# Plain k-tiles between the pair operations of a group, and a fifth pair of buffers for split weights

## The chip, the cores and the metric

The kernel runs on one core of a Trainium2 chip. The metric is the device time of one execution in microseconds (us); it took 2559.11 us in the median of three runs (2558.76 to 2559.23). TensorE (PE) multiplies matrices, VectorE (DVE) and ScalarE (ACT) work elementwise, GpSimd (POOL) does little here, and SyncE (SP) issues the loads of the weights. Each engine executes its own instructions in the order in which they stand.

## The reference

Two transformer blocks follow one another on 256 tokens of width 2048, everything in float32. The change touches the output projection and the gated feed-forward network (FFN) of the first block:

```
D_FF = -(-8 * D_MODEL // (3 * 256)) * 256          # 5632
...
        mixed = g_a * (y_a @ w_branch_a[l]) + g_b * (y_b @ w_branch_b[l])
        h = h + mixed @ w_out[l]

        hn = rmsnorm(h, ffn_norm[l])
        h = h + (jax.nn.silu(hn @ w_gate[l]) * (hn @ w_up[l])) @ w_down[l]
    return rmsnorm(h, final_norm)
```

Ahead of it stand the first block's norm, input projection and two attentions; behind it the whole second block, which the change leaves as it is.

## The kernel before

**Products in three passes.** A float32 operand is split into a high half (rounded to the fast float32r type) and a low half (what is left), and a product is taken as high x high + high x low + low x high: three matmuls. For weights, `high` (L449) makes the high half `wh` on ACT, and `low` (L453) the low half `wl` on DVE, each on a tile of 128 x 1024.

**The stream of weights.** `STREAM` lists all weight tiles in the order of use. `fetch` loads a tile into one of six `raw` buffers, in order on SP's queue. `divide` splits the next one; `fill` keeps `look` split tiles ready ahead of the one in use (2 in the output projection, 3 in the FFN), in four pairs of `wh` and `wl` buffers. `low` of a tile is recorded one tile after its `high`.

**A group** (`group_t`, matmuls on L578) makes 1024 output columns for all 256 tokens in four blocks: two halves of the tokens by two halves of the columns, in eight PSUM banks. The stage has 19 groups: two of the output projection (`out`), then in three parts 4, 4 and 3 groups of gate and up (`gu`), each part followed by two groups of `down`. A k-tile is 128 rows of the weights. For four of the k-tiles, taken as two pairs, a group forms the 2 x 2 x 2 block product with seven products instead of eight, in the manner of Strassen and Winograd. These seven operations (`OPS`: B11, B22, t1, t3, t2, B21, t4) have 6 matmuls each; `t1`, `t3`, `t2` and `t4` need a sum of two weight tiles first, which DVE makes in place (L431). The other k-tiles (12 in most groups, 8 in the last two) are plain: 12 matmuls and one split tile each, four products that accumulate into the banks B21, B22, t4 and std.

In the kernel before, a group runs its seven operations first and all plain k-tiles after them. When `t4` is recorded, `early` takes the banks B11, t1, t3 and t2 into sums (L616 on ACT, L617 to L620 on DVE; in `out` and `down` these are added to the residual `h`, L632); after the last plain k-tile `late` adds the other four banks (L1156 in `gu`, L636 in `out` and `down`). Then the roles of the banks are permuted (`map`), so that the next group opens in banks which `early` has freed.

**Tasks.** Small work between groups is held in generators that are resumed every 2400 ns of recorded matmul work: `turned` transposes a group's result four 128 x 128 blocks at a time (L649) into one bank, `self.one`, and hands it to `done`, which evacuates it as split operands (L478, L479, L481, L482). For `gu`, `gated` first multiplies silu(gate) by up (L1128, L1129). A task is brought to its end by `finish`: after the next group in `out` and `gu`, before the last four k-tiles in `down`.

A scheduler then puts the recorded instructions of each engine into their final order, by priority and by when it expects them to be ready.

Of the kernel before, what the change touches and what calls it, by code (L numbers as in the profile page):

```python
# [14 lines left out]
ALU = mybir.AluOpType  # L15
# [15 lines left out]
OUT_PAIRS = ((0, 1), (2, 3))  # L31
GU_PAIRS = ((0, 4), (1, 5))
DOWN_PAIRS = ((0, 1), (2, 3))
# [16 lines left out]
DV_COLS = ((0, 330), (330, 676), (676, 1024))  # L50


def weight_plan():
    plan = []

    def unit(key, *segs):
        plan.append((key, segs))
# [9 lines left out]
    def tgroup(key, w, kts, pairs, col):  # L67


        kts = list(kts)  # L70
        w1, w2 = (w, w) if isinstance(w, str) else w
        c1 = [(col, col + 512)]
        c2 = [(col + 512, col + 1024)] if isinstance(w, str) else c1
        for c in range(0, len(pairs), 2):
# [5 lines left out]
        rest = [k for i, k in enumerate(kts) if not any(i in p for p in pairs)]  # L80
        for i in range(0, len(rest), 2):
            unit(key + ("std", i), *[x for k in rest[i:i + 2] for x in ((w1, [k], c1), (w2, [k], c2))])

    for c in range(8):
        unit(("lat", c), ("w_in", [2 * c, 2 * c + 1], [(3072, 3840)]))
# [25 lines left out]
    for j in range(2, 16):  # L111
        if j < 10:
            h = j - 2
# [27 lines left out]
    for p, (i0, n) in enumerate(PARTS):  # L141
# [7 lines left out]
    return plan  # L149


def _width(ranges):
    return sum((b if a is None else b - a) for a, b in ranges)


PLAN = weight_plan()
# [6 lines left out]
OPS = ("B11", "B22", "t1", "t3", "t2", "B21", "t4")  # L163

ROLES = {"B11": 0, "B22": 1, "t1": 2, "t3": 3, "t2": 4, "B21": 5, "t4": 6, "std": 7}
EARLY, LATE = (0, 2, 3, 4), (1, 5, 6, 7)


def stream():

    out, u = [], 0
    while u < len(PLAN):
        key, n = PLAN[u][0], UNIT_COLS[u]
        if key[0] == "lat":
            u += 1
        elif "pair" in key:
            out += [(op, u, n // 2) for op in OPS]
            u += 2
        else:
            cuts = [n // 2, n] if key[0] in ("va", "dv") else [min(a + 1024, n) for a in range(0, n, 1024)]  # L180
            out += [(u, a, b) for a, b in zip([0] + cuts, cuts)]
            u += 1
    return out


# [66 lines left out]
class Norm:  # L252

    r = B = None
# [14 lines left out]
class Prog:  # L269
# [282 lines left out]
        nc.vector.tensor_tensor(o[:, 1], f, o[:, 0].bitcast(F32), op=ALU.subtract)  # L552
        return o

    def group_t(self, key, xs, cs, pairs, early, late, extra=None):

        nc = self.nc  # L560
        n = len(xs)
        paired = {k for p in pairs for k in p}
        rest = [k for k in range(n) if k not in paired]
        b = {}
        place = lambda r: self.psp.tile([P, 512], F32, tag=f"bank{self.map[ROLES[r]]}", name="q", bufs=1)
        self.one = self.map[7]
        left = dict.fromkeys(OPS, 3 * len(pairs))
        std = (("B21", "B22"), ("t4", "std"))
        left["std"] = 0
        for r in std[0] + std[1]:  # L570
            left[r] += 3 * len(rest)
# [12 lines left out]
        for c in range(0, len(pairs), 2):  # L584
            for op in OPS:
                p, wh, wl = self.take()
                assert p[0] == op and PLAN[p[1]][0] == key + ("pair", c, 0), (key, p)
                self.fill()
                for i, (ka, kb) in enumerate(pairs[c:c + 2]):
                    w = [h[:, 512 * i:512 * i + 512] for h in (wh, wl)]  # L590
                    cmb = lambda m: (cs[c + i][:, 0, m, :], cs[c + i][:, 1, m, :])
                    x = {"B11": lambda: cut(xs[ka], t0), "B21": lambda: cut(xs[kb], t0), "B22": lambda: cmb(2),
                         "t4": lambda: cut(xs[kb], t1), "t1": lambda: cmb(0), "t2": lambda: cmb(1),
                         "t3": lambda: cmb(3)}[op]()
                    product(op, x, w)
        if pairs:
            early(b)
        self.one = self.map[4]
        for i, k in enumerate(rest):
            if extra:  # L600
                extra(k)
            p, wh, wl = self.take()
            assert PLAN[p[0]][0][:len(key)] == key, (key, p)
# [472 lines left out]
    def block1_out(self, mixed, cm):  # L1076

        nc = self.nc
# [16 lines left out]
        task = None  # L1095
        for g in range(2):
            early, late = self.residual(h, g)
            self.group_t(("out", g), mixed, cm, OUT_PAIRS, early, late)
            if task:
                self.finish(task)  # L1100
# [6 lines left out]
            task = self.add(self.turned(src, 8, (lambda g: lambda i, x: done(8 * g + i, x))(g), 3), urgent=True)  # L1107
        m = self.small()
        nc.vector.reduce_sum(m, ss, axis=AX.X)
        nh = Norm()  # L1110
# [3 lines left out]
    def block1_ffn(self, h, hn, cs, nh, th):  # L1114
# [30 lines left out]
        for p, (i0, n) in enumerate(PARTS_T):  # L1145
            acts, ca, task = [], [], th
            for g in range(i0 // 4, (i0 + n) // 4):
                sb_ = []

                def early(b):  # L1150
                    sb_.extend(self.sums(b))

                def late(b):
                    for i, r in enumerate(self.LATE_OF):
                        if sb_:
                            nc.vector.tensor_tensor(sb_[i], b[r], sb_[i], op=ALU.add)  # L1156
                        else:
                            sb_.append(b[r])

                self.group_t(("gu", g), hn, cs, GU_PAIRS, early, late)  # L1160
                self.finish(task)
# [3 lines left out]
            t0, need = task, n - 4  # L1165
            for g in range(2):
                early, late = self.residual(h, g)
                operands = Acts(acts, n)
                self.group_t(("down", p, g), operands, ca, DOWN_PAIRS, early, late,
                             lambda k: k >= need and self.finish(t0))  # L1170
                if last:
                    src = [h[t][:, 1024 * g:1024 * g + 1024] for t in range(2)]

# [373 lines left out]
    def build(self):  # L1547
        nc, tc, t = self.nc, self.tc, self.t
        with ExitStack() as ctx:
# [20 lines left out]
            with ExitStack() as c0:  # L1570
# [94 lines left out]
```

## Time and profile before

| | us |
|---|---|
| median of three runs | 2559.11 |
| the profiled execution | 2559.29 |
| its span | 2557.5 |
| PE busy (matmuls) | 2495.7 (98%) |
| weight loads of PE (PEld) | 2129.2 (83%) |
| DVE busy | 1841.6 (72%) |
| ACT busy | 1366.4 (53%) |
| stage of the groups, first to last matmul | 522.3 to 1361.8 |

A row of the profile names line, engine, operation, output and inputs, shapes and a count; in square brackets stands the idle time of the engine ahead of it and what ended that. Matmuls overlap, so one lasts longer than the interval between two.

### The profile page before, as it was taken

Reading aid. Unit: us, or ns where it says so; the run is one execution under the profiler, and the core shown is the slowest. Engines: PE = TensorE matmul, PEld = TensorE weight load, DVE = VectorE, ACT = ScalarE, POOL = GpSimd, SP = SyncE. Lnnn points to the kernel's source line nnn. Section 1 sums busy time; section 2 is a strip of 40 time slices with the busy share of each in tenths; the row PEclk is TensorE's granted clock in tenths of the full one; section 3 lists DMA queues with packets and bytes.
Section 4 is the critical chain, followed back from the end, with each engine's and each line's share of the span. In section 5 each row is a group of like instructions: output and inputs, shape, how many; then the busy total and the mean of one; then the engine's idle time right before and its main releaser. Section 6 shows DMA issues by size and latency. Waiting matters only on the chain.

```text
span 2557.5 us, 35199 instructions
## 1 busy us (share of the span) xinstructions
PE 2495.7 (98%) x13218; PEld 2129.2 (83%) x13218; DVE 1841.6 (72%) x2617; ACT 1366.4 (53%) x2036; POOL 119.3 (5%) x134
## 2 busy tenths in 40 slices
PE   9999999999999999999998999999999999999997
PEld 8988888877877777787777888888788888888886
DVE  8867766888787877878786578665876566656765
ACT  6555565556554454545456545555655455545553
POOL 3000000000000000000004000002200000000002
PEclk9999999999999999999999999999999999999998
DMA  6644455556555564565644544455455555555552
GB/s 235 202 153 146 165 180 183 189 198 207 172 181 201 169 204 167 184 210 170 205 166 144 197 164 157 146 190 175 148 188 183 190 190 190 184 193 191 186 176 91
DMA packets 131723, 458.46 MB, mean 179 GB/s; under 512 B 14624, under 2 KB 17056, under 8 KB 131296
## 3 DMA queue, kind: packets, MB, share of 16 engines
q1 hardware_dynamic: 130608, 452.78, 52.6%
q10 hardware_dynamic: 944, 3.43, 0.4%
q8 instruction: 103, 1.69, 0.3%
q14 instruction: 68, 0.56, 0.1%
HBM read 454.06 MB, written 2.10 MB: 178 GB/s over the span
## 4 chain that ended last, share of the span: by engine, by line
PE 85%; DVE 10%; issue 2%; ACT 2%; DMA 0%; POOL 0%; POOLq 0%; ACTq 0%; SPq 0%; DVEq 0%
PE acc L494 33%; PE q L578 23%; PE acc L495 17%; DVE wl L453 4%; PE acc L492 2%; PE acc L527 2%; PE acc L526 2%; PE acc L528 1%; DVE raw L431 1%; PE acc L491 1%; ACT wh L449 1%; PE ms L770 1%; DVE ft L1156 1%; DVE hl L482 1%; PE ms L1326 1%
## 5 line engine op out<-in xcount | busy, mean ns | idle before, releaser
L453 DVE TENSOR_TENSOR wl<-raw,wh 128x1024 fp32r<-128x1024 f32 (+4 forms) x939 | 1116.0, 1198 | 536.4 <-ACT wh L449 532.8
L449 ACT ACTIVATE wh<-raw 128x1024 fp32r<-128x1024 f32 (+4 forms) x939 | 961.5, 1032 | 813.2 <-PE acc L494 344.2
L494 PE MATMUL acc<-hl,wh 128*128 128x512 f32 x3746 | 1327.3, 397 | 7.4 <-DVE hl L482 6.5
L495 PE MATMUL acc<-hl,wl 128*128 128x256 f32 x3746 | 1049.0, 281 | 0.7 <-DVE wl L453 0.7
L494 PEld LDWEIGHTS acc<-hl,wh 128*128 128x128 f32 x3746 | 703.5, 188 | 166.9 <-DVE hl L482 6.0
L495 PEld LDWEIGHTS acc<-hl,wl 128*128 128x128 f32 x3746 | 708.2, 189 | 9.2 <-DVE wl L453 2.0
L578 PE MATMUL q<-wh,hl 128*128 128x512 f32 x1988 | 628.4, 392 | 18.5 <-ACT wh L449 17.9
L578 PEld LDWEIGHTS q<-wh,hl 128*128 128x128 f32 x1988 | 372.0, 188 | 107.5 <-ACT wh L449 30.8
L578 PE MATMUL q<-wl,hl 128*128 128x512 f32 x994 | 388.6, 391 | 0.9 <-DVE wl L453 0.8
L578 PEld LDWEIGHTS q<-wl,hl 128*128 128x128 f32 x994 | 186.7, 188 | 41.7 <-DVE wl L453 2.6
L657 ACT ACTIVATE ev<-acc 128x256 f32<-128x256 f32 x288 | 106.3, 384 | 182.6 <-PE acc L492 181.3
L690 POOL TENSOR_TENSOR ssq<-ssq,sq 128x256 f32<-128x256 f32 x77 | 74.9, 982 | 1562.1 <-ACT sq L680 1560.4
L660 DVE TENSOR_TENSOR tmp<-acc,ev 128x256 f32<-128x256 f32 x257 | 101.4, 422 | 60.0 <-ACT ev L657 59.8
L492 PE MATMUL acc<-hl,wh 128*128 128x512 f32 x288 | 108.3, 396 | 0.0
L578 PE MATMUL q<-wh,combo 128*128 128x512 f32 x304 | 100.8, 396 | 4.2 <-ACT wh L449 4.2
L526 PE MATMUL acc<-wh,hl 128*128 128x512 f32 (+4 forms) x264 | 94.0, 356 | 2.8 <-ACT hl L481 2.3
L527 PE MATMUL acc<-wl,hl 128*128 128x512 f32 (+4 forms) x264 | 91.0, 346 | 3.1 <-DVE wl L453 2.4
L431 DVE TENSOR_TENSOR raw<-raw 128x1024 f32<-128x1024 f32 x76 | 92.8, 1221 | 1.3
L528 PE MATMUL acc<-wh,hl 128*128 128x512 f32 (+4 forms) x264 | 89.4, 344 | 0.6 <-DVE hl L482 0.6
L491 PE MATMUL acc<-hl,wl 128*128 128x256 f32 x288 | 82.9, 288 | 0.0
L578 PEld LDWEIGHTS q<-wh,combo 128*128 128x128 f32 x304 | 57.1, 188 | 19.1 <-ACT wh L449 6.6
L578 PE MATMUL q<-wl,combo 128*128 128x512 f32 x152 | 60.7, 399 | 0.2 <-DVE wl L453 0.2
(275 smaller groups left out, 1625.0 us busy)
## 6 DMA issues: line engine op xcount, KB each, us to landing
raw<-in_w_dram SPq DMA_DIRECT2D x801, 512.0 KB, 4.0
raw<-in_w_dram SPq DMA_DIRECT2D x18, 384.0 KB, 3.2
raw<-in_w_dram SPq DMA_DIRECT2D x16, 362.0 KB, 4.2
raw<-in_w_dram SPq DMA_DIRECT2D x16, 346.0 KB, 3.4
raw<-in_w_dram SPq DMA_DIRECT2D x15, 256.0 KB, 3.6
raw<-in_w_dram SPq DMA_DIRECT2D x8, 364.0 KB, 3.8
raw<-in_w_dram SPq DMA_DIRECT2D x8, 348.0 KB, 3.7
x<-in_xT_dram SPq DMA_DIRECT2D x8, 256.0 KB, 5.8
```

What stands on the lines that cost most here:

```text
L431: self.nc.vector.tensor_tensor(raw[:, :n], parts[a][:, :n], parts[b][:, :n], op=ALU.add)
L449: self.nc.scalar.activation(wh[:, :n], raw[:, :n], AF.Copy)
L453: self.nc.vector.tensor_tensor(wl[:, :n], raw[:, :n], wh[:, :n].bitcast(F32), op=ALU.subtract)
L491: nc.tensor.matmul(acc[:, S:], wl, x[:, 0, :], start=False, stop=False)
L492: nc.tensor.matmul(acc, wh, x, start=False, stop=True)
L494: nc.tensor.matmul(acc, wh, x, start=first, stop=False)
L495: nc.tensor.matmul(acc[:, S:], wl, x[:, 0, :], start=False, stop=last)
L526: nc.tensor.matmul(acc, xh, wh, start=(k == 0), stop=False)
L527: nc.tensor.matmul(acc, xh, wl, start=False, stop=False)
L528: nc.tensor.matmul(acc, xl, wh, start=False, stop=(k == n - 1))
L578: nc.tensor.matmul(b[r], x[i], w[j], start=left[r] == total[r], stop=left[r] == 1)
L657: nc.scalar.activation(e, acc[:, S:], AF.Copy)
```

## The change

Within a group of two pairs, `group_order` puts three plain k-tiles in front of t2 and one in front of B21; the others follow t4 as before. `weight_plan` returns this order for each group, and the stream of weights and `group_t` go by it. A plain k-tile writes its two column halves in the order 1, 0, and the late adds go B22, B21, std, t4. Transposes now use the bank that t2 takes (`self.one`), wait for two resumptions instead of three, and must be finished before t2. `early` runs when t4 is recorded. A pool `wx1` adds a fifth pair of `wh` and `wl` buffers for the stage; `look` is 4 in the FFN, and 3 in the last group, without the fifth pair. Each engine has as many instructions as before.

```diff
+def group_order(npairs, rest):
+    rest, out = list(rest), []
+    for c in range(0, npairs, 2):
+        for op in OPS:
+            if op == "t2" and c == 0:
+                out += [rest.pop(0) for _ in range(3)]
+            elif op in ("t1", "t3", "t2") and c or op == "B21":
+                out.append(rest.pop(0))
+            out.append((c, op))
+    return out + rest
...
-    def group_t(self, key, xs, cs, pairs, early, late, extra=None):
+    def group_t(self, key, xs, cs, pairs, early, late, tasks=()):
...
-        self.one = self.map[7]
+        self.one = self.map[ROLES["t2"]]
...
-        for c in range(0, len(pairs), 2):
-            for op in OPS:
-                p, wh, wl = self.take()
...
-        if pairs:
-            early(b)
-        self.one = self.map[4]
-        for i, k in enumerate(rest):
-            if extra:
-                extra(k)
+        for step in ORDERS[key]:
             p, wh, wl = self.take()
             self.fill()
-            for t, ts in enumerate((t0, t1)):
-                for m in range(2):
-                    product(std[t][m], cut(xs[k], ts), [h[:, 512 * m:512 * m + 512] for h in (wh, wl)])
+            if isinstance(step, int):
+                for t, ts in enumerate((t0, t1)):
+                    for m in (1, 0):
+                        product(std[t][m], cut(xs[step], ts), [h[:, 512 * m:512 * m + 512] for h in (wh, wl)])
+                continue
+            c, op = step
+            if op == "t2":
+                self.finish(*tasks)
...
+            if op == "t4" and not left["t2"]:
+                early(b)
+                self.one = self.map[ROLES["t3"]]
         late(b)
         self.map = [self.map[i] for i in EARLY + LATE]
-        self.one = self.map[7]
+        self.one = self.map[ROLES["t2"]]
...
+    LATE_IN = (1, 0, 3, 2)
...
-            for a, r in zip(at, self.LATE_OF):
-                nc.vector.tensor_tensor(a, b[r], a, op=ALU.add)
+            for i in self.LATE_IN:
+                nc.vector.tensor_tensor(at[i], b[self.LATE_OF[i]], at[i], op=ALU.add)
...
-        self.look, self.ahead = 3, True
+        self.look, self.ahead = 4, True
...
-            yield from self.turned(z, 4, done, 3)
+                if last and g:
+                    self.wx, self.look = None, 3
...
-                    t0 = self.add(self.turned(src, 8, done, 3), urgent=True)
+                    t0 = self.add(self.turned(src, 8, done, 2), urgent=True)
...
+                    self.wx, self.wxn = c2.enter_context(tc.tile_pool(name="wx1", bufs=1)), 1
```

DVE at the boundary between two `gu` groups, in the kernel before; the first row ends the plain k-tiles of one group, `ft` rows on L1156 are its late adds, `z` its gate products:

```order
L453 TENSOR_TENSOR wl<-raw,wh 128x1024 x11
L431 TENSOR_TENSOR raw<-raw 128x1024 x2
L453 TENSOR_TENSOR wl<-raw,wh 128x1024
L1156 TENSOR_TENSOR ft<-q,ft 128x512
L453 TENSOR_TENSOR wl<-raw,wh 128x1024
L1156 TENSOR_TENSOR ft<-q,ft 128x512 x3
L1129 SCALAR_TENSOR_TENSOR z<-ft,small,z 128x512 x2
L431 TENSOR_TENSOR raw<-raw 128x1024
L453 TENSOR_TENSOR wl<-raw,wh 128x1024 x3
L431 TENSOR_TENSOR raw<-raw 128x1024
L479 TENSOR_TENSOR hl<-tr,hl 128x256
L617 TENSOR_TENSOR ft<-q,ft 128x512
```

The same place now (the low half is L475, the sum of weights L453, the late add L1169, the gate product L1146, the evacuation of a transpose L501):

```order
L475 TENSOR_TENSOR wl<-raw,wh 128x1024 x6
L453 TENSOR_TENSOR raw<-raw 128x1024 x2
L475 TENSOR_TENSOR wl<-raw,wh 128x1024 x2
L453 TENSOR_TENSOR raw<-raw 128x1024
L1169 TENSOR_TENSOR ft<-q,ft 128x512 x2
L475 TENSOR_TENSOR wl<-raw,wh 128x1024
L1169 TENSOR_TENSOR ft<-q,ft 128x512 x2
L1146 SCALAR_TENSOR_TENSOR z<-ft,small,z 128x512
L475 TENSOR_TENSOR wl<-raw,wh 128x1024
L1146 SCALAR_TENSOR_TENSOR z<-ft,small,z 128x512
L475 TENSOR_TENSOR wl<-raw,wh 128x1024 x3
L501 TENSOR_TENSOR hl<-tr,hl 128x256
```

Three of the four sums of weights now stand ahead of the late adds; before, two did, and the early sums (L617) of the new group began right behind the fourth.

DVE at the end of the last group, before; L636 are the late adds to `h`, `wl` of 692 columns belong to the stage that follows, L482 evacuates transposes:

```order
L453 TENSOR_TENSOR wl<-raw,wh 128x692 x2
L482 SCALAR_TENSOR_TENSOR hl<-tr,gfp,hl 128x256 x2
L636 TENSOR_TENSOR h_5506<-q,h_5506 128x512 x2
L636 TENSOR_TENSOR h_5507<-q,h_5507 128x512
L453 TENSOR_TENSOR wl<-raw,wh 128x692
L636 TENSOR_TENSOR h_5507<-q,h_5507 128x512
L453 TENSOR_TENSOR wl<-raw,wh 128x692 x5
```

The same place now (early sums L635 to L638, adds to `h` L651, late adds L655):

```order
L635 TENSOR_TENSOR ft<-q,ft 128x512
L655 TENSOR_TENSOR h_5511<-q,h_5511 128x512
L636 TENSOR_TENSOR ft<-q,ft 128x512
L475 TENSOR_TENSOR wl<-raw,wh 128x692
L637 SCALAR_TENSOR_TENSOR ft<-q,ft 128x512
L638 TENSOR_TENSOR ft<-q,ft 128x512
L651 TENSOR_TENSOR h_5511<-h_5511,ft 128x512
L651 TENSOR_TENSOR h_5512<-h_5512,ft 128x512 x2
L655 TENSOR_TENSOR h_5511<-q,h_5511 128x512
L655 TENSOR_TENSOR h_5512<-q,h_5512 128x512 x2
L475 TENSOR_TENSOR wl<-raw,wh 128x692 x3
```

The early sums of the last group have come to its end, since its t2 waits for the transposes to leave the bank; on PE, t2's 6 matmuls now stand 13 matmuls before the group's end, and the first transposes of the result 37 matmuls of the next stage behind it (48 before).

## Rows read from the trace of the kernel before

**Rows 1.** Stretches: start and end, us, busy us of engines, PEclk, DMA.

```profile
522.30:1361.80 839.50, 814.31 (x3575) 656.30 (x3574) 666.46 (x750) 434.00 (x529) 15.65 (x15) 1.00 0.56 188
```

**Rows 2.** Line L578, group matmuls: ns min/median/max, first and last start.

```profile
L578 PE MATMUL q<-wh,hl x1988: 387/389/507, 522.3 to 1361.6; 128*128 128x512 f32 x199
...
L578 PEld LDWEIGHTS q<-wh,hl x1988: 185/188/193, 522.1 to 1361.4; 128*128 128x128 f32 x199
...
L578 PE MATMUL q<-wl,hl x994: 387/389/502, 522.6 to 1361.4; 128*128 128x512 f32 x199
...
L578 PE MATMUL q<-wh,combo x304: 388/392/505, 523.7 to 1332.8; 128*128 128x512 f32 x152
...
L578 PE MATMUL q<-wl,combo x152: 388/394/503, 523.9 to 1332.6; 128*128 128x512 f32 x152
```

**Rows 3.** Chain that ended last: start us, us, piece; its longest unbroken run.

```profile
850.72 42.30 PE q L578 x185
```

**Rows 4.** PE in order of time (start us, us), around four transposes.

```profile
629.84 0.62 PE L578 MATMUL q<-wh,hl 128*128 128x512 f32 x2
630.30 0.60 PE L649 MATMUL tr<-cc,h 128*128 128x128 f32 x4
...
630.96 0.62 PE L578 MATMUL q<-wh,hl 128*128 128x512 f32 x2
```

**Rows 5.** Waits of PE, 522 to 1362: us in total, times, longest.

```profile
PE q L578 <- ACT wh L449: 22.1, 43, 0.8
PE tr L649 <- ACT res L1181: 1.1, 2, 0.7
PE q L578 <- DVE wl L453: 1.0, 2, 0.8
```

**Rows 6.** PE in order of time: waits in four groups.

```profile
708.49 0.50 PE L578 MATMUL q<-wh,combo 128*128 128x512 f32 x1 [0.44 <-ACT wh L449]
...
754.09 0.50 PE L578 MATMUL q<-wh,combo 128*128 128x512 f32 x1 [0.44 <-ACT wh L449]
...
1119.49 0.40 PE L578 MATMUL q<-wh,hl 128*128 128x512 f32 x1
1120.65 0.50 PE L578 MATMUL q<-wh,hl 128*128 128x512 f32 x1 [0.77 <-ACT wh L449]
1121.60 0.96 PE L578 MATMUL q<-wh,hl 128*128 128x512 f32 x3 [0.45 <-ACT wh L449]
...
1350.08 0.66 PE L649 MATMUL tr<-cc,h 128*128 128x128 f32 x4 [0.71 <-ACT res L1181]
```

**Rows 7.** DVE in order of time, at a boundary between two gate/up groups.

```profile
703.01 1.88 DVE L1156 TENSOR_TENSOR ft<-q,ft 128x512 f32<-128x512 f32 x3
704.81 1.41 DVE L1129 SCALAR_TENSOR_TENSOR z<-ft,small,z 128x512 f32<-128x512 f32 x2
...
707.27 3.56 DVE L453 TENSOR_TENSOR wl<-raw,wh 128x1024 fp32r<-128x1024 f32 x3
710.75 1.22 DVE L431 TENSOR_TENSOR raw<-raw 128x1024 f32<-128x1024 f32 x1
```

**Rows 8.** Groups by form, 522.3 to 1361.8: busy us, mean ns | idle before.

```profile
L449 ACT ACTIVATE wh<-raw 128x1024 fp32r<-128x1024 f32 x350 | 363.3, 1057 | 384.9 <-PE q L578 291.6 <-DVE raw L431 75.2 <-issue 12.7
...
L479 DVE TENSOR_TENSOR hl<-tr,hl 128x256 fp32r<-128x256 f32 x44 | 18.3, 417 | 0.0
...
L649 PE MATMUL tr<-cc,z 128*128 128x128 f32 x88 | 13.2, 272 | 0.0
...
L649 PE MATMUL tr<-cc,h 128*128 128x128 f32 x48 | 7.5, 278 | 1.4 <-ACT res L1181 1.1 <-DVE ft L617 0.3
```

**Rows 9.** DMA issues, 522 to 1362: KB each, median us to landing.

```profile
raw<-in_w_dram SPq DMA_DIRECT2D x290, 512.0 KB, 4.9
```

**Rows 10.** PE in order of time: matmuls of the stage behind the groups.

```profile
1369.40 0.32 PE L527 MATMUL acc<-wl,hl 128*128 128x346 f32 x1
1369.56 0.32 PE L528 MATMUL acc<-wh,hl 128*128 128x346 f32 x1
```

More of the change, by code (lines that the diff above doesn't have):

```diff
@@ L50 @@
 DV_COLS = ((0, 330), (330, 676), (676, 1024))
+OPS = ("B11", "B22", "t1", "t3", "t2", "B21", "t4")
+ROLES = {"B11": 0, "B22": 1, "t1": 2, "t3": 3, "t2": 4, "B21": 5, "t4": 6, "std": 7}
+EARLY, LATE = (0, 2, 3, 4), (1, 5, 6, 7)
+def group_order(npairs, rest):
[8 more added lines that the diff above has]
+    return out + rest
 def weight_plan():
-    plan = []
+    plan, orders = [], {}
     def unit(key, *segs):
@@ L73, in tgroup @@
         c2 = [(col + 512, col + 1024)] if isinstance(w, str) else c1
+        rest = [k for k in range(len(kts)) if not any(k in p for p in pairs)]
         for c in range(0, len(pairs), 2):
@@ L79, in tgroup @@
             unit(key + ("pair", c, 1), *seg(w2, ka, c2), *seg(w1, kb, c1))
-        rest = [k for i, k in enumerate(kts) if not any(i in p for p in pairs)]
         for i in range(0, len(rest), 2):
-            unit(key + ("std", i), *[x for k in rest[i:i + 2] for x in ((w1, [k], c1), (w2, [k], c2))])
+            unit(key + ("std", i), *[x for k in rest[i:i + 2] for x in ((w1, [kts[k]], c1), (w2, [kts[k]], c2))])
+        orders[key] = group_order(len(pairs), rest)
     for c in range(8):
@@ L148, in weight_plan @@
             group(("fo", p, g), "w_ffn_out_2", range(i0, i0 + n), [(256 * g, 256 * g + 256)])
-    return plan
+    return plan, orders
 def _width(ranges):
     return sum((b if a is None else b - a) for a, b in ranges)
-PLAN = weight_plan()
+PLAN, ORDERS = weight_plan()
 UNIT_OF = {key: i for i, (key, _) in enumerate(PLAN)}
 UNIT_COLS = [sum(len(kts) * _width(rr) for _, kts, rr in segs) for _, segs in PLAN]
-OPS = ("B11", "B22", "t1", "t3", "t2", "B21", "t4")
-ROLES = {"B11": 0, "B22": 1, "t1": 2, "t3": 3, "t2": 4, "B21": 5, "t4": 6, "std": 7}
-EARLY, LATE = (0, 2, 3, 4), (1, 5, 6, 7)
 def stream():
-    out, u = [], 0
+    out, u, seen = [], 0, set()
     while u < len(PLAN):
         key, n = PLAN[u][0], UNIT_COLS[u]
[L174 to L179, printed above, removed]
+        of = key[:-2] if "std" in key else key[:-3] if "pair" in key else None
+        if of in ORDERS:
+            if of not in seen:
+                seen.add(of)
+                i = 0
+                for x in ORDERS[of]:
+                    if isinstance(x, int):
+                        v = UNIT_OF[of + ("std", i // 2 * 2)]
+                        out.append((v, 1024 * (i % 2), 1024 * (i % 2) + 1024))
+                        i += 1
+                    else:
+                        v = UNIT_OF[of + ("pair", x[0], 0)]
+                        out.append((x[1], v, UNIT_COLS[v] // 2))
+        elif key[0] != "lat":
             cuts = [n // 2, n] if key[0] in ("va", "dv") else [min(a + 1024, n) for a in range(0, n, 1024)]
             out += [(u, a, b) for a, b in zip([0] + cuts, cuts)]
-            u += 1
+        u += 1
     return out
@@ L570, in group_t @@
         for r in std[0] + std[1]:
-            left[r] += 3 * len(rest)
+            left[r] += 3 * (len(xs) - 2 * len(pairs))
         total = dict(left)
@@ L583, in group_t @@
         cut = lambda x, ts: (x[:, 0, ts], x[:, 1, ts])
-        for c in range(0, len(pairs), 2):
-            for op in OPS:
-                p, wh, wl = self.take()
[L587 to L595, printed above, removed]
@@ L596, in group_t @@
-        if pairs:
-            early(b)
-        self.one = self.map[4]
-        for i, k in enumerate(rest):
-            if extra:
-                extra(k)
+        for step in ORDERS[key]:
             p, wh, wl = self.take()
-            assert PLAN[p[0]][0][:len(key)] == key, (key, p)
             self.fill()
-            for t, ts in enumerate((t0, t1)):
-                for m in range(2):
-                    product(std[t][m], cut(xs[k], ts), [h[:, 512 * m:512 * m + 512] for h in (wh, wl)])
+            if isinstance(step, int):
+                assert PLAN[p[0]][0][:len(key)] == key, (key, p)
+                for t, ts in enumerate((t0, t1)):
[3 more added lines that the diff above has]
+            c, op = step
+            assert p[0] == op and PLAN[p[1]][0] == key + ("pair", c, 0), (key, p)
+            if op == "t2":
+                self.finish(*tasks)
+            for i, (ka, kb) in enumerate(pairs[c:c + 2]):
+                w = [h[:, 512 * i:512 * i + 512] for h in (wh, wl)]
+                cmb = lambda m: (cs[c + i][:, 0, m, :], cs[c + i][:, 1, m, :])
+                x = {"B11": lambda: cut(xs[ka], t0), "B21": lambda: cut(xs[kb], t0), "B22": lambda: cmb(2),
+                     "t4": lambda: cut(xs[kb], t1), "t1": lambda: cmb(0), "t2": lambda: cmb(1),
+                     "t3": lambda: cmb(3)}[op]()
+                product(op, x, w)
+            if op == "t4" and not left["t2"]:
+                early(b)
+                self.one = self.map[ROLES["t3"]]
@@ L1097, in block1_out @@
             early, late = self.residual(h, g)
-            self.group_t(("out", g), mixed, cm, OUT_PAIRS, early, late)
-            if task:
-                self.finish(task)
+            self.group_t(("out", g), mixed, cm, OUT_PAIRS, early, late, [task] if task else ())
             for t in range(2):
@@ L1106, in block1_out @@
             src = [h[t][:, 1024 * g:1024 * g + 1024] for t in range(2)]
-            task = self.add(self.turned(src, 8, (lambda g: lambda i, x: done(8 * g + i, x))(g), 3), urgent=True)
+            task = self.add(self.turned(src, 8, (lambda g: lambda i, x: done(8 * g + i, x))(g), 2), urgent=True)
         m = self.small()
@@ L1148, in block1_ffn @@
                 sb_ = []
-                def early(b):
-                    sb_.extend(self.sums(b))
                 def late(b):
[L1154 to L1161, printed above, removed]
+                    for i in self.LATE_IN:
+                        nc.vector.tensor_tensor(sb_[i], b[self.LATE_OF[i]], sb_[i], op=ALU.add)
+                self.group_t(("gu", g), hn, cs, GU_PAIRS, lambda b: sb_.extend(self.sums(b)), late, [task] if task else ())
                 task = self.add(gated(sb_, acts, ca), urgent=True)
@@ L1164, in block1_ffn @@
             last = p == len(PARTS_T) - 1
-            t0, need = task, n - 4
+            t0 = task
             for g in range(2):
+                if last and g:
+                    self.wx, self.look = None, 3
                 early, late = self.residual(h, g)
                 operands = Acts(acts, n)
-                self.group_t(("down", p, g), operands, ca, DOWN_PAIRS, early, late,
-                             lambda k: k >= need and self.finish(t0))
+                self.group_t(("down", p, g), operands, ca, DOWN_PAIRS, early, late, [t0])
                 if last:
```

3 lines of the change are left out of this document (removed).

## The prediction

> **What bounds the kernel now.** I read first the view of stretches, to find the stage that the change touches. From the first matmul of the attention's output projection to the last of the first FFN, 522.3 to 1361.8 us, TensorE (PE) is busy 814.3 of 839.5 us, at a granted clock of 1.00; VectorE (DVE) has 666 us of work, ScalarE (ACT) 434 [rows 1]. So the matmuls set the pace, and the question is how much of the stage is not matmul.
>
> The counts of the matmul line give 1988 + 994 + 304 + 152 = 3438 matmuls of 128x512, the first at 522.3, the last at 1361.6 [rows 2]. Their price without a wait comes from the longest unbroken run in the chain of work: 185 in 42.30 us, 228.6 ns each [rows 3]. So 3438 cost 785.9 us. Four transposes between matmuls: from the matmul at 630.07 (second of its row) to the second one behind them at 630.96 are 0.89 us, less two intervals 0.43 [rows 4]. The stage has 34 such fours (88 + 48 transposes [rows 8]), 14.6 us. Together 800.5 us, so **39.0 us of the stage are lost**.
>
> The waits say where: PE waited 43 times for a high half (ACT, L449), 22.1 us, and twice for a low half (DVE, L453), 1.0 us; two are at transposes (ACT, L1181), 1.1, and two more fill up the 25.2 idle us [rows 5]. A wait costs more than its idle time, since matmuls overlap: with 0.77 idle the start at 1120.65 is 1.16 after the one before, 0.93 over the interval; with 0.45 the next is 0.72 over [rows 6]. That is 0.22 more for each of 49, so 25.2 + 10.8 = 36.0; 3.0 I cannot place.
>
> The profile's busy time alone would put the most that can be won at 25.2 us. The Trainium skill (Perfetto Trace Analysis, Identifying the Most-Contended Engine) calls matmul busy time a poor measure of headroom and the share of weight loading a good one. By that, 656.3 us of loads at 188 ns per 228.6 (82.2%) fill 798 us and leave 41, so the trace agrees with the page; by busy time the forecast below would be 14 us later, 2545.
>
> Why PE waits: one gate/up group has its first wait at 708.49, the next its own at 754.09, a period of 45.60 us [rows 6] against 186 x 0.2286 + 2 x 0.43 = 43.4. The first seven operations are 42 matmuls, 9.6 us. DVE needs for them 4 sums (t1, t3, t2, t4) and 7 low halves, 11 instructions of 1.16 us (three from 707.27 to the next row's start at 710.75), 12.8 us; and in the same time come 4 late adds at 0.61 and 2 gate products at 0.70 [rows 7], together 16.6. Three operations split ahead cover part of the 7 us between; some 2.2 us a group are left. ACT stood 75.2 us for those sums [rows 8].
>
> **The change, part by part.** The engines keep the same number of instructions; nothing is saved, all is order.
>
> *Plain k-tiles between.* A group now runs B11, B22, t1, t3, three plain k-tiles, t2, one plain, B21, t4, then the rest. A plain k-tile is 12 matmuls, 2.74 us, for one low half of 1.16; a sum operation 6 matmuls, 1.37 us, for two DVE instructions, 2.3. I follow DVE in its new order over a boundary between two gate/up groups, T being the end of the group before. B11, B22 and the sums for t1, t3 and t2 are done before T. The first bank closes 9 matmuls before T; its late add and the next: from -1.9 to -0.7; low t3 to 0.5; two late adds to 1.7; product z to 2.4; low of plain 0 to 3.6; second z to 4.3; lows of plain 1, 2 and t2 to 5.5, 6.7, 7.9. PE wants t3 at 4.1, plain 0 at 5.9 (behind one four of transposes), plain 1 at 8.7, plain 2 at 11.4, t2 at 14.6 (behind a second four). Margins 3.6, 2.3, 3.2, 4.7, 6.7 us. Later t4 is wanted at 20.1 and split by 15. So the waits for splits go, all but the start of the first projection group, where the splits are made while the branch stage still loads DVE: two waits as at 1120.65 and 1121.60 [rows 6] are 1.65, so 0 to 1.65; I take 1.0.
>
> *Fifth buffer pair, four splits ahead.* No instruction more; it is what lets t3 and plain 0 lie ready at T, and counted in the margins. In the last group it is gone and look-ahead falls back to three.
>
> *Transposes.* They move into the bank that t2 takes next, start two pumps after the boundary instead of three, and must be through before t2. The first four need both z: ready at 4.3, used at 5.5. The second four need the first evacuated: DVE does hl (0.42 [rows 8]), low of plain 3, hl, to 9.9; PE comes 17 matmuls behind the first four, at 5.5 + 0.43 + 3.9 = 9.8. That is the thinnest place: 11 groups, 0 to 0.9 us each (the wait at 1350.08 idles 0.71 [rows 6], plus 0.22); by the chain 0.1, I take 0.2, 2.2 us. The second projection group and the first gate/up group have four fours with gains and combinations to make: 8 x 0.3 = 2.4, bounds 0 to 7.2.
>
> *The last group and what follows.* Its transposes (four fours, 8 ACT evacuations each) hold back t2, which the order now puts 13 matmuls before the end. Each four may wait as at 1350.08 [rows 6], so 0 to 3.7; I take 2.0. Behind t2 DVE has four sums, four h adds, four late adds at 0.61 and one low half of 346 columns x2 (0.8): 8.1 us, plus 0.2 to start. PE covers it with 7 matmuls (1.6) and 37 of the next stage at 0.16 [rows 10], 5.9: 7.5. The next four then waits 0.8, and the split behind the chain 0.6 more: 1.4 added, bounds 0 to 2.8. Before, the early sums lay far ahead of this point.
>
> *Order of the late adds, and which product of a plain k-tile comes first.* Same instructions; they close the bank first that t2's transposes need. Nothing, as long as the late adds end at 1.7 and the first write behind them is plain 0 at 5.9; without that cover up to 0.7 a group, counted in the first rival.
>
> *Loads.* Three of six raw buffers hold B11, B22, B12 for longer, until t2 and t4. SP issues in order: plain 3 goes out when t3 is split (0.5), B21 when plain 0 is (3.6), and lands 4.9 later [rows 9], 8.5; the sum for t4 wants it on DVE at 9.9. Nothing; margin 1.4.
>
> **Sum.** Left of the 39.0: 1.0 + 2.2 + 2.4 + 2.0, and half of the unplaced 3.0, 1.5: 9.1 us. 39.0 - 9.1 - 1.4 = 28.5 us saved. The profiled run took 2559.29 (span 2557.5), so 2530.8; the median of the runs is 0.2 lower, which leaves **2531 us**.
>
> **Rivals.**
> 1. *The transposes' one bank takes the place of the waits removed.* Each second four waits in full (11 x 0.93 = 10.2), all 12 in the three heavy groups too (11.2), the first group keeps 1.65, the unplaced 3.0 stay, the end costs 2.8: 28.9 left, 10 saved, 2549. For it: the wait at 1350.08 is just this, ACT behind its queue of splits. Against: the chain above meets the second four within 0.1. The Trainium skill (Perfetto Trace Analysis, Matmuls) wants independent groups to rotate through banks so that evacuation overlaps, which speaks against this change; no row here has both arrangements.
> 2. *It does not do what it says:* ACT's high halves follow PE's release of a buffer (291.6 us of its idle time) and the four sums stay in ACT's way (75.2) [rows 8], so waits only move from the start of a group to t2 and t4. Then 2559. Against: margins of 2 to 7 us where 2.2 were missing, and DVE at 79%.
> 3. *Slower: loads starve.* With three raw buffers held, DVE stops at the sum for t4 until B21 has landed, and the evacuations of the second four and low B21 stand behind it. From a landing of 4.9 + 1.4 on DVE waits; the second four is evacuated by 12.2 and t2 begins at 14.6, so from about 8.7 PE waits as well. At 11 us it loses 2.3 in each of 19 groups, 44 us: 28.5 - 44, 2575. For it: SP already queues behind DVE. Against: the median of 290 loads, and DMA engines 56% busy.
>
> **How the numbers follow.** Forecast 0.74, its own range 2521 (nothing left) to 2541 (twice as much left); rival 1 0.16; rival 2 0.06; rival 3 0.04. 2521 to 2549 leaves out rivals 2 and 3 and the edges of the others. What can be told from no change is 0.2%, 5 us: the forecast and rival 1 are faster, 0.90; rival 2 mostly same, 0.06; slower 0.04.
>
> **What would show it.** Right: the stage ends near 1331; a group's period falls from 45.6 to 43.4 to 43.8; PE's waits for high halves in the stage fall from 43 to under 8; the matmul interval stays 228.6 ns. The last stage's first transposes wait about 1 us. Rival 1: PE's waits at transposes for ACT or DVE rise from two to over ten. Rival 2: as many waits for high halves, at t2 and t4. Rival 3: DVE waits for DMA at the sums. I would be wrong if the interval itself grew under the denser work of DVE and ACT, or if the granted clock left 1.00 in the stage.

## The result: 2526.05 us, and the profile after

| | before | after |
|---|---|---|
| median of 4 runs, us | 2559.16 | 2526.05 |
| lowest to highest, us | 2558.76 to 2559.23 | 2525.97 to 2526.22 |
| ratio, 95% interval | | 0.9871 [0.9854, 0.9888] |
| span of the profiled execution, us | 2557.5 | 2524.3 |
| stage of the groups, us | 839.5 | 807.1 |
| behind the stage to the end of the span, us | 1195.7 | 1195.1 |

The change saves 33.1 us; 28.5 were forecast. In the changed kernel the group matmuls are on L597, the high halves on L471, the low halves on L475, the sums of weights on L453, the transposes on L668.

The view of stretches of the changed kernel, of the stage and of the first 38.2 us behind it (columns as in [rows 1]):

```profile
522.10:1329.20 807.10, 805.18 (x3575) 656.93 (x3574) 662.98 (x743) 440.25 (x529) 14.65 (x15) 1.00 0.59 195
...
1329.20:1367.40 38.20, 32.42 (x180) 27.90 (x180) 22.57 (x46) 23.52 (x52) 14.39 (x19) 0.96 0.40 129
```

Beside [rows 1], DVE and ACT have nearly the same work, and PE idles 1.9 us where it idled 25.2. PE's waits from 515 to 1345 us of the changed kernel (us in total, times, longest):

```profile
PE q L597 <- DVE wl L475: 1.5, 2, 1.2
PE tr L668 <- ACT res L1192: 1.1, 2, 0.7
PE acc L548 <- ACT hl L503: 1.0, 1, 1.0
```

The 43 waits for a high half [rows 5] are gone. What is left, from PE in order of time: one in the first group of the output projection, one in the first gate/up group, one at transposes in the last group, and two behind the stage:

```profile
533.66 0.50 PE L597 MATMUL q<-wl,hl 128*128 128x512 f32 x1 [1.17 <-DVE wl L475]
...
638.36 0.50 PE L597 MATMUL q<-wl,hl 128*128 128x512 f32 x1 [0.30 <-DVE wl L475]
...
1321.12 0.66 PE L668 MATMUL tr<-cc,h 128*128 128x128 f32 x4 [0.35 <-ACT res L1192]
...
1340.10 0.43 PE L548 MATMUL acc<-wh,hl 128*128 128x346 f32 x1 [0.95 <-ACT hl L503]
1342.05 0.89 PE L668 MATMUL tr<-cc,h 128*128 128x128 f32 x4 [0.74 <-ACT res L1192]
```

PE waited behind the stage before the change too. The first waits there in the kernel before, and in each kernel the same later row, which begins 30.6 us behind the stage's end before and 30.0 now:

```profile
1371.11 0.43 PE L526 MATMUL acc<-wh,hl 128*128 128x346 f32 x1 [0.80 <-ACT hl L481]
1373.53 0.43 PE L526 MATMUL acc<-wh,hl 128*128 128x346 f32 x1 [0.89 <-ACT hl L481]
...
1392.37 0.60 PE L698 MATMUL ms<-ones,ssq 128*128 128x1 f32 x4 [0.69 <-POOL ssq L690]
```

```profile
1359.23 0.60 PE L717 MATMUL ms<-ones,ssq 128*128 128x1 f32 x4 [0.69 <-POOL ssq L709]
```

Of the 34 fours of transposes, only the one in the last group waits for its one bank. The groups by form show who was relieved (busy, mean ns | idle before):

```profile
L471 ACT ACTIVATE wh<-raw 128x1024 fp32r<-128x1024 f32 x350 | 370.0, 1060 | 318.1 <-PE q L597 291.7 <-DVE wl L475 7.6 <-issue 4.8
```

ACT's 75.2 us of waiting for DVE's sums [rows 8] is gone, while its 291.6 us of waiting for PE to free a buffer stays, 291.7: that one was never a cost. The chain that ended last (start us, us, piece):

```profile
797.79 124.80 PE q L597 x545
...
927.03 39.39 PE q L597 x172
...
970.09 40.01 PE q L597 x175
...
1014.63 39.33 PE q L597 x171
...
1058.29 122.69 PE q L597 x535
```

From 927.03 to 1058.29 are three periods of a gate/up group, 43.75 us each (45.60 before). But the long runs give 124.80 / 545 = 229.0 and 122.69 / 535 = 229.3 ns a matmul, where [rows 3] gave 228.6. This small difference became the main question.

**Where it sits.** I took from the trace the time from each group matmul's start to the next one's, where it is under 320 ns, and sorted these intervals by the buffer pair that held the weights, which the addresses in the program's memory layout tell. Before: all pairs 227.9 to 228.6 ns. After: three pairs 228.5 to 229.2, **the fifth pair 233.6** (647 intervals), the pair that mostly follows it 230.2 (679). The trace shows it without any sorting. PE in order of time in the changed kernel; the rows shown are the turns from one plain k-tile to the next, 12 matmuls apart, and the fifth pair is in use between the second and the third:

```profile
896.55 0.62 PE L597 MATMUL q<-wh,hl 128*128 128x512 f32 x2
...
899.27 0.62 PE L597 MATMUL q<-wh,hl 128*128 128x512 f32 x2
...
902.06 0.62 PE L597 MATMUL q<-wh,hl 128*128 128x512 f32 x2
...
904.81 0.62 PE L597 MATMUL q<-wh,hl 128*128 128x512 f32 x2
```

They are 2.72, 2.79 and 2.75 us apart. Over the stage: 647 x (233.6 - 228.8) + 679 x (230.2 - 228.8) = 3.1 + 1.0 = 4.1 us. With the waits, 2.8 us over 11 gaps of 320 ns and more, the floor of 800.5 gives 807.4; measured 807.1.

### The profile page after: what moved, and what is told of

It is laid out like the page before. It is cut to its first block, busy times and chain, and to the rows that moved or that the text cites. A ratio compares the mean times of both kernels' runs of the same rounds, so it can differ in the third digit from the quotient of the medians.

```text
span 2524.3 us, 35146 instructions
## 1 busy us (share of the span) xinstructions
PE 2485.4 (98%) x13218; PEld 2128.2 (84%) x13218; DVE 1842.0 (73%) x2617; ACT 1372.8 (54%) x2036; POOL 118.2 (5%) x134
## 4 chain that ended last, share of the span: by engine, by line
PE 94%; DVE 4%; ACT 1%; issue 1%; POOL 0%; DMA 0%; POOLq 0%; SPq 0%; ACTq 0%; DVEq 0%
PE acc L516 33%; PE q L597 30%; PE acc L517 17%; PE acc L514 3%; PE acc L549 2%; PE acc L548 2%; PE acc L550 2%; PE acc L513 1%; PE ms L789 1%; DVE wl L475 1%; PE tr L668 1%; DVE hl L504 1%; PE ms L1337 1%; PE ms L818 1%; ACT wh L471 0%
## 5 line engine op out<-in xcount | busy, mean ns | idle before, releaser
L475 DVE TENSOR_TENSOR wl<-raw,wh 128x1024 fp32r<-128x1024 f32 (+4 forms) x939 | 1116.1, 1196 | 499.8 <-ACT wh L471 495.8
L471 ACT ACTIVATE wh<-raw 128x1024 fp32r<-128x1024 f32 (+4 forms) x939 | 968.2, 1033 | 748.1 <-PE acc L516 344.7
L597 PE MATMUL q<-wh,hl 128*128 128x512 f32 x1988 | 624.3, 392 | 0.0
L597 PEld LDWEIGHTS q<-wh,hl 128*128 128x128 f32 x1988 | 372.2, 188 | 80.4 <-ACT wh L471 0.4
L597 PE MATMUL q<-wl,hl 128*128 128x512 f32 x994 | 389.8, 392 | 1.5 <-DVE wl L475 1.5
L597 PEld LDWEIGHTS q<-wl,hl 128*128 128x128 f32 x994 | 186.5, 188 | 42.1 <-DVE wl L475 2.3
L597 PE MATMUL q<-wh,combo 128*128 128x512 f32 x304 | 101.4, 395 | 0.0
L453 DVE TENSOR_TENSOR raw<-raw 128x1024 f32<-128x1024 f32 x76 | 93.0, 1224 | 1.9
L597 PEld LDWEIGHTS q<-wh,combo 128*128 128x128 f32 x304 | 57.1, 188 | 14.7 <-PE q L597 0.6
L597 PE MATMUL q<-wl,combo 128*128 128x512 f32 x152 | 60.0, 395 | 0.0
```

What stands on the lines that cost most here:

```text
L471: self.nc.scalar.activation(wh[:, :n], raw[:, :n], AF.Copy)
L475: self.nc.vector.tensor_tensor(wl[:, :n], raw[:, :n], wh[:, :n].bitcast(F32), op=ALU.subtract)
```

## Experiments

Each was measured beside the kernel before, whose medians were 2558.84 to 2559.69 us. None leaves anything out of the computation.

### Which part does it? Order alone, buffers alone

`e1_order_alone` is the changed kernel with four pairs and three tiles ahead:

```diff
-                    self.wx, self.wxn = c2.enter_context(tc.tile_pool(name="wx1", bufs=1)), 1
-        self.look, self.ahead = 4, True
+        self.look, self.ahead = 3, True
```

> The changed kernel with four buffer pairs and three splits ahead, as before: the order of the plain k-tiles (with its banks and transposes) alone. Theory A (DVE falls behind only in the burst of sums, and the plain k-tiles between spread it): one split less takes 1.4 to 2.7 us from margins of 2.3 to 6.7 us, so most of the 33 us stay: 2527 to 2533 us. Rival B (the fourth split ahead pays for half of it): 2538 to 2546 us.

Measured: 2520.42 us (2519.56 to 2520.84), ratio 0.9848 [0.9833, 0.9862]: **5.6 us faster than the whole change**, and below both expectations. The stage, and PE's waits inside it (522.1 to 1323.8), of this kernel:

```profile
522.10:1323.70 801.60, 801.16 (x3576) 656.63 (x3574) 661.89 (x743) 437.94 (x529) 14.74 (x15) 1.00 0.59 196
```

```profile
PE tr L668 <- ACT res L1192: 0.3, 1, 0.3
```

No group matmul waits, and the interval is 228.5 to 228.9 ns in all pairs.

`e2_buffers_alone` is the kernel before, in its old order, with the fifth pair and four tiles ahead:

```diff
+                    self.wx, self.wxn = c2.enter_context(tc.tile_pool(name="wx1", bufs=1)), 1
-        self.look, self.ahead = 3, True
+        self.look, self.ahead = 4, True
+                if last and g:
+                    self.wx, self.look = None, 3
```

> The kernel before with the fifth buffer pair and four splits ahead, its order kept. Theory A: one more operation (1.4 us of TensorE) lies ready at a boundary where about 2.2 us a group are missing, and DVE has the time for it beforehand; at most 19 x 1.4 = 26 us are won, and as the burst itself stays, 8 to 26: 2533 to 2551 us, with waits left at the plain k-tiles that follow t4. Rival B (look-ahead is what counts): all of it, 2526 to 2531 us. If buffers do nothing: 2559 us.

Measured: 2527.08 us (2525.68 to 2527.74), ratio 0.9873 [0.9859, 0.9888]. Its waits from 515 to 1345 us:

```profile
PE acc L526 <- ACT hl L481: 1.7, 2, 0.9
PE q L578 <- ACT wh L449: 1.1, 2, 0.7
PE tr L649 <- ACT res L1183: 0.4, 2, 0.2
```

Theory A, that the burst in the old order would stay, falls: one more split tile ahead also takes 43 waits to 2. Each half of the change removes what there was to remove, and together they don't add up. That fits the prediction's own shortage of 2.2 us a group: a plain k-tile more in store is 2.74 us of matmuls. The fifth pair is slow here too (233.5 ns).

### Is it DVE's burst? The sums made twice as long

Each sum of weights is followed by a second operation of the same size on the same tile, which leaves its values as they are; `e3` on the kernel before, `e4` on the changed one:

```diff
+                 self.nc.vector.tensor_tensor(raw[:, :n], raw[:, :n], raw[:, :n], op=ALU.max)
```

> The kernel before with a second DVE instruction of the same size behind each sum of two weight tiles (the maximum of the tile with itself, so nothing changes in the result): 4 x 1.16 = 4.6 us more DVE work in each group, 76 instructions, 88 us in all. Theory A: in the burst it lies on the path in full, 60 to 88 us: 2619 to 2647 us. Rival (the waits come from ACT's buffers or from the banks, not from DVE's burst): under 20 us, below 2580.

> The changed kernel with the same second instruction behind each sum. Theory A: the margins of 2 to 7 us take it up, 0 to 10 us lost: 2526 to 2536 us. Rival (the changed order is itself at the edge of DVE, 79 to 89% busy): 20 to 60 us lost, 2546 to 2586.

`e3`: 2685.29 us (2680.96 to 2686.07), ratio 1.0488 [1.047, 1.0505], 126 us more. Its stage, and PE's waits there:

```profile
522.30:1487.50 965.20, 858.66 (x3575) 673.08 (x3574) 751.94 (x826) 439.25 (x529) 15.67 (x15) 0.97 0.49 164
```

```profile
PE q L579 <- ACT wh L450: 84.9, 84, 4.2
PE q L579 <- DVE wl L454: 16.2, 16, 1.3
```

DVE has 76 instructions more and is 78% busy, so by the mean there was room; yet PE loses more than DVE's 76 x 1.22 = 93 us, and more than theory A allowed (60 to 88). The line named is ACT's, but ACT does nothing new: it waits for DVE's sums (100.7 us, against 75.2 in [rows 8]). PE's idle time grew by 81 us (106.5 against 25.2). The clock was lost at times as well, which no theory had: the granted clock in the stage is 0.97, and 103 matmuls, each lot behind waits, run at some 426 ns instead of 229, which is 20 us. Overlap lost at some 54 more waits (0.22 each) gives 12; another 12 I cannot place.

`e4`: 2540.70 us (2539.49 to 2541.49), ratio 0.9927 [0.9912, 0.9942], 14.6 us over the changed kernel. Its stage and the largest waits:

```profile
522.00:1344.00 822.00, 811.83 (x3587) 659.40 (x3586) 741.81 (x818) 433.02 (x529) 17.22 (x15) 1.00 0.57 192
```

```profile
PE q L598 <- ACT wh L472: 3.8, 5, 1.1
PE q L598 <- DVE hl L505: 2.9, 1, 2.9
```

The same extra work costs 126 us when it comes in a burst and 15 when it is spread; DVE is 90% busy here and still hides most of it. Expected by theory A were 0 to 10, by the rival 20 to 60: between, nearer to A. So DVE's burst is the cause of the waits, and the spread order is a reserve against it; what belongs to the burst, `e5` shows.

### How much mixing is needed?

Three orders on the base of `e1` (four pairs, three ahead). `e5`: four plain k-tiles first, then the seven operations in a row. `e6`: two plain k-tiles in front of t2 and none in front of B21. `e8`: one each in front of t3, t2, B21 and t4.

```diff
 e5
-    rest, out = list(rest), []
+    rest, out = list(rest[4:]), list(rest[:4])
...
-            if op == "t2" and c == 0:
-                out += [rest.pop(0) for _ in range(3)]
-            elif op in ("t1", "t3", "t2") and c or op == "B21":
-                out.append(rest.pop(0))
 e6
-                out += [rest.pop(0) for _ in range(3)]
-            elif op in ("t1", "t3", "t2") and c or op == "B21":
+                out += [rest.pop(0) for _ in range(2)]
+            elif op in ("t1", "t3", "t2") and c:
 e8
-            if op == "t2" and c == 0:
-                out += [rest.pop(0) for _ in range(3)]
-            elif op in ("t1", "t3", "t2") and c or op == "B21":
+            if op in ("t3", "t2", "B21", "t4"):
                 out.append(rest.pop(0))
```

> The changed kernel with four buffer pairs and three splits ahead, and four plain k-tiles in front of the seven operations, none between them. Theory A (the sums must be spread): the seven operations stand in a row again, DVE needs 12.8 us for TensorE's 9.6, waits come back at t2 and t4 in every group, 2532 to 2550 us. Rival C (the burst only hurts where it meets the late adds, gate products and evacuations of the boundary, which now fall beside plain k-tiles; three operations split ahead cover 4.6 of the 12.8 us): 2520 to 2526 us.

> The same with two plain k-tiles in front of t2 and none before B21 (instead of three and one). Theory A: two give TensorE 5.5 us more beside the burst, where some 2.2 us a group are missing, so no wait for splits comes back: 2520 to 2524 us. If the count of four was needed: 2528 to 2540 us.

> Four buffer pairs, three splits ahead, and one plain k-tile in front of each of t3, t2, B21 and t4. Theory A: the sums are spread as evenly as they can be; nothing left to win against three and one, 2519 to 2523 us. If the transposes get in the way (they must be through before t2, which comes one k-tile after t3): 2524 to 2532 us, with waits at transposes.

| | us | ratio, 95% interval |
|---|---|---|
| `e5`, none between | 2528.07 (2527.38 to 2529.89) | 0.9881 [0.9866, 0.9896] |
| `e6`, two between | 2523.81 (2523.48 to 2524.29) | 0.9864 [0.9848, 0.988] |
| `e1`, four between in two places | 2520.42 (2519.56 to 2520.84) | 0.9848 [0.9833, 0.9862] |
| `e8`, four between in four places | 2520.30 (2519.92 to 2520.46) | 0.9849 [0.9835, 0.9864] |

The waits of `e5` in the stage:

```profile
PE q L593 <- ACT wh L467: 2.5, 7, 0.9
PE q L593 <- DVE wl L471: 1.7, 1, 1.7
PE tr L664 <- ACT res L1188: 0.9, 1, 0.9
```

Theory A wanted 2532 or more for `e5` and missed; rival C wanted 2526 or less. Its seven operations stand in a row as before the change; what differs is that DVE's work at the group's boundary now falls beside plain k-tiles: in the trace all 22 gate products start there (none before), and 52 of the 76 sums of weights (36 before). That is worth 30.8 us, together with the transposes' bank and the order of the late adds, which `e5` shares with the change and which were not tried apart. Mixing adds 7.7 more, of which two plain k-tiles bring 4.3. Where the four stand does not matter (`e1`, `e8`). In none of them do transposes wait more than once in the stage's groups, though the bank and the time left for it differ.

### Why is the fifth pair slow?

All on the changed kernel. `e7` opens the pair's pool ahead of the others of the stage; `e9` keeps the fifth pair and splits only three tiles ahead; `e10` puts the pool at the other end of the memory; `e11` and `e12` put 64 and 192 unused bytes in front of it.

```diff
 e7
+                    self.wx, self.wxn = c2.enter_context(tc.tile_pool(name="wx1", bufs=1)), 1
                     self.hp = c2.enter_context(tc.tile_pool(name="hp", bufs=1))
...
-                    self.wx, self.wxn = c2.enter_context(tc.tile_pool(name="wx1", bufs=1)), 1
 e9
-        self.look, self.ahead = 4, True
+        self.look, self.ahead = 3, True
 e10
-                    self.wx, self.wxn = c2.enter_context(tc.tile_pool(name="wx1", bufs=1)), 1
+                    self.wx, self.wxn = c2.enter_context(tc.tile_pool(name="wx1", bufs=1, side="right")), 1
 e11 (e12 has 48 in place of 16)
+                    gap = c2.enter_context(tc.tile_pool(name="gap", bufs=1)).tile([P, 16], F32, name="gap")
+                    nc.gpsimd.memset(gap, 0.0)
```

> The changed kernel, its fifth buffer pair kept, but its pool opened ahead of the pools of the residual and the sums, so that it lies elsewhere in SBUF. In the changed kernel matmuls on the fifth pair start 233.5 ns apart, on the other four 228 to 229. Theory P (it is the place): the fifth pair's interval changes, towards 228.5, and 3 to 5 us are won: 2521 to 2523 us. Rival N (a fifth pair costs this anywhere): 233 ns again, 2526 us.

> The changed kernel with its five pairs, but with the split only three tiles ahead in FFN 1 instead of four. In the changed kernel matmuls that read the fifth pair follow one another in 233.6 ns, those of the other four pairs in 228.6 to 229.0. Theory A: it is the place of the fifth pair (or that it is a pool of its own) that costs; then with three ahead its interval stays at 233 to 234.5, the stage is 806 to 808 and the time 2525 to 2527. Theory B: it is the greater look-ahead, VectorE and ScalarE writing while TensorE reads; then the interval falls to under 230, and the time goes to 2520 to 2522, that of the order alone.

> The changed kernel with the fifth pair's pool opened at the other end of the memory. Theory A, the place costs: the fifth pair's interval changes from 233.6 to 231 or less, and the time goes down by 2 us or more, to 2520 to 2524. Rival B, any fifth pair costs, whatever its place: 233 to 234.5 ns and 2525 to 2527 again.

> The changed kernel with 64 unused bytes in front of the fifth pair, which then begins at the same place within 1024 bytes as the other four pairs (992; it was 928, and in the run with its pool opened earlier 896, both slow; at the other end of the memory it was 992 and fast). Theory A: what costs is the place within a span of 128 to 1024 bytes, not the end of the memory; then the fifth pair's interval falls from 233.6 to 228.5 to 229.5 and the time is 2520 to 2523. Rival B: it is the end of the memory, or the neighbours there; then 233 to 234.5 ns and 2525 to 2527.

> The same with 192 unused bytes: the fifth pair begins at 96 within 1024 bytes and within 256, at 96 within 128 bytes as the other pairs do. If theory A holds with spans of 128 bytes: 228.5 to 229.5 ns and 2520 to 2523. If the span is 256 bytes or longer, or B holds: 233 to 234.5 ns and 2525 to 2527.

The other four pairs all begin at 992 within 1024 bytes of their partition, and so do the buffers `hl` of the plain stationary operands. "Begins" is where the fifth pair lies by the program's memory layout.

| | begins, mod 1024 | interval of the fifth pair, ns | us | ratio, 95% interval |
|---|---|---|---|---|
| changed kernel | 928 | 233.6 | 2526.05 | 0.9871 [0.9854, 0.9888] |
| `e9`, three ahead | 928 | 233.8 | 2526.35 (2525.49 to 2527.43) | 0.9869 [0.9853, 0.9886] |
| `e7`, pool opened first | 896 | 234.1 | 2526.16 (2525.80 to 2527.28) | 0.9873 [0.9859, 0.9888] |
| `e12`, 192 bytes up | 96 | 233.4 | 2525.50 (2525.39 to 2527.27) | 0.9870 [0.9854, 0.9887] |
| `e10`, other end | 992 | 228.8 | 2521.35 (2521.15 to 2521.73) | 0.9851 [0.9836, 0.9866] |
| `e11`, 64 bytes up | 992 | 228.8 | 2521.78 (2521.48 to 2522.73) | 0.9854 [0.9839, 0.9869] |

PE in order of time in `e11`, at the same turns as above, the fifth pair again between the second and the third row:

```profile
895.14 0.61 PE L597 MATMUL q<-wh,hl 128*128 128x512 f32 x2
...
897.86 0.61 PE L597 MATMUL q<-wh,hl 128*128 128x512 f32 x2
...
900.58 0.61 PE L597 MATMUL q<-wh,hl 128*128 128x512 f32 x2
...
903.30 0.61 PE L597 MATMUL q<-wh,hl 128*128 128x512 f32 x2
```

2.72 us three times. One run of the chain that all kernels have shows the same; of `e11`, and of `e12`:

```profile
1055.87 121.88 PE q L597 x535
```

```profile
1058.13 122.54 PE q L597 x535
```

`e9` clears the look-ahead: DVE and ACT running further ahead is not what slows the matmuls. `e10` and `e11` clear the fifth pair as such. `e7` had pointed the wrong way: another place, as slow, as its rival N said. What decides is where the pair begins: at the offset of the other pairs it costs nothing, at three other offsets some 5 ns a matmul. `e12` shares that offset within 128 bytes (96) but not within 256, and is slow, so if a place within some span counts, the span is longer than 128 bytes. With the pair moved 64 bytes the changed kernel is 4.3 us faster; the intervals gave 4.1. Why an offset slows the reading stays open, and so does whether the place itself counts or its distance from the other operand. In the changed kernel the 36 intervals in which the fifth pair (928) meets a combination of the gate/up groups, which begins at 928 too, have a median of 227 ns, the 551 beside `hl` (992) one of 233; but in `e7` 60 intervals with both at 896 have 231.

`e8` and `e1`, at 2520.3 and 2520.4 us, beat both kernels: the new order without the fifth pair. At the good offset the pair still costs 1.4 us (`e11` against `e1`). The trace of `e11` has two waits for low halves, 1.35 us in the first projection group and 0.29 in the first gate/up group:

```profile
PE q L597 <- DVE wl L475: 1.6, 2, 1.4
```

The changed kernel, `e7`, `e9`, `e10` and `e12` have the same two, and neither `e1` nor `e8` has one; so of the 5.6 us between the change and `e1` some 4.3 are the offset, and these waits can account for the rest. Why a fifth pair brings them stays open.

## Why the prediction was right, and where it was not

- **What bounds the stage: right.** By starts of matmuls 39.0 us of the stage were lost; `e1` wins back 38 of them (801.6 against 839.5), with the same loads of weights, 656.6 us. Busy time, which left 25.2, is refuted by this: what matmuls lose by not overlapping is in no idle time. The Trainium skill (Perfetto Trace Analysis, Identifying the Most-Contended Engine) puts the load share above busy time as a measure of headroom. By the loads 41 us were to be had, so the run agrees with it.
- **Why PE waited: right.** `e3` and `e4` show DVE's burst as the cause, `e5` that the sums hurt where they meet the boundary's other work, as the prediction's 16.6 us of DVE work beside 9.6 of matmuls had it. [rows 8] named it already: ACT idle for DVE's sums.
- **Which edit removes the waits: half right.** "It is what lets t3 and plain 0 lie ready at T" is wrong of the fifth pair. `e1` has no wait of a group matmul without it, and `e2` two without the new order. Margins of 2 to 7 us where 2.2 were missing should have told that either half is enough.
- **The fifth pair at nothing: this step failed.** "No instruction more" was true, and no cover was named since none seemed needed; it measured 4.1 us by the intervals and 4.3 by `e11`, and 1.4 more in waits that `e1` does not have. "The matmul interval stays 228.6 ns" holds, to 0.6 ns, for three pairs of the five. The text named a grown interval as what would prove it wrong, but laid it to denser work of DVE and ACT; `e9` shows it is not that.
- **Transposes: mis-sized.** 2.2 + 2.4 us were left for them; the trace shows no wait of transposes in those groups. The chain of the prediction gave 0.1 at the thinnest place, and the 0.2 taken was its caution. Its start of two resumptions holds only for the projection and the last two groups: in `gated` the three stay, and the line that the section on the change shows as taken out is still there. Rival 1 is refuted. The Trainium skill (Perfetto Trace Analysis, Matmuls) wants independent groups to rotate through banks, which the prediction held against the change; here the one bank for all fours cost no wait but that of 0.35 us in the last group.
- **The last group and what follows: mis-sized.** 2.0 and 1.4 were taken. One wait of 0.35 us is left in the group, and what follows is 0.6 us shorter than before. The forecast wait of about 1 us at the next stage did come (0.95 and 0.74), but in place of waits that were there before (0.80 and 0.89), so it was no cost of the change.
- **The start of the output projection:** 1.0 taken, 1.2 idle in one wait; but it is the wait that comes with the fifth pair, and `e1` has none. **The unplaced 3.0**, of which half was kept, went with the waits.
- **Loads:** DVE never waited for a load of weights in the stage (once, 1.4 us, for the tokens), with the DMA engines 59% busy; rival 3 is out, rival 2 too.

The sum: of 10.5 us forecast as left or added, 2.8 of waits stayed and 0.6 were gained behind the stage; the fifth pair's slower intervals, 4.1 and not in the forecast, took about half of the difference back. So two errors of opposite sign leave 2526 where 2531 stood: that the number came so close is in part luck. Without the second the time is that of `e11`, 2521.8, 9 us under the forecast and near the low end of its own range.

## What to carry to other kernels

When an engine off the critical path falls behind only in bursts, one more buffer or a better order may do the same job: try each alone before both, since the second cure brings only its cost. A buffer is not free because it adds no instruction: after adding one, compare the interval of the instructions that read it with that of the others, start to start, and if it is longer, shift the buffer to the others' offset. Count what is to be won by starts, not by idle time.

## What was not expected of the hardware

- The place of a matmul's 128x512 moving operand changes its pace: 228.8 ns where the buffer began at 992 within 1024 bytes, as its neighbours did, 233.4 to 234.1 at 928, 896 and 96. The median duration of all the stage's matmuls, 389 ns, hides it; only when they are sorted by pair does it show, 394 to 395 for the slow pair against 389. The buffers of `combo`, the stationary operand of 456 matmuls of the stage, begin at 928 in the gate/up groups and at 896 in the others, and these matmuls follow one another more slowly too: in `e1` 230.5 and 233.6 ns in the mean, against 228.3 for the others. Moving them was not tried, so that their offset is the cause is not shown.
- With 104 waits of PE of up to 4.2 us (`e3`) the granted clock of the stage was 0.97, and 103 matmuls took 426 ns, about twice their interval, as at 1.2 GHz in place of 2.4. The length of one wait does not decide it: in `e4` eight matmuls ran at 427 ns behind two waits of 0.81 and 0.75 us at 527 us, and none did behind its wait of 2.9 us at 641. In the kernel before, with waits of 0.8 us at most, the clock stayed at 1.00.
